# First unit of a seven-product feed-forward: weight sums split between GpSimd and VectorE, and the sixth product's left side built with one operation per token pair

## The chip, the cores and the metric

The kernel runs on one core of a Trainium2 chip, in one launch. The time is the device time of one execution in microseconds (us); the kernel before takes 2167.95 us, the median of three runs (2166.27 to 2169.98). Engines are named as in the profile: PE is TensorE (PEld its weight loads), DVE is VectorE, ACT is ScalarE, POOL is GpSimd, SP is SyncE, which issues most of the transfers.

## The reference, cut to what matters

Two layers of a decoder trunk on 512 tokens of width 1024, all float32:

```python
for l in range(DEPTH):                                   # DEPTH = 2
    x = x + 0.5 * swiglu_ffn(rmsnorm(x, ffn1_norm[l]), ffn1_w_gate[l], ffn1_w_up[l], ffn1_w_down[l])
    z = rmsnorm(x, mix_norm[l]) @ w_in[l]                # -> S5, pooling and conv groups -> y
    x = x + y @ w_out[l]
    x = x + cross_attention(rmsnorm(x, xattn_norm[l]), rmsnorm(mem, mem_norm[l]), wq, wk, wv, wo)
    x = x + 0.5 * swiglu_ffn(rmsnorm(x, ffn2_norm[l]), ffn2_w_gate[l], ffn2_w_up[l], ffn2_w_down[l])
return rmsnorm(x, final_norm)

def rmsnorm(x, g):
    return x * rsqrt(mean(x * x, axis=-1) + EPS) * g
def swiglu_ffn(h, w_gate, w_up, w_down):                 # 1024 -> 2816 -> 1024
    return (silu(h @ w_gate) * (h @ w_up)) @ w_down
```

The change concerns three of the four feed-forward blocks: `ffn2` of both layers and `ffn1` of the second. The first block of the program is built in another way and is not touched.

## The kernel before

Every float32 matrix product is done as three products of rounded parts: an operand is split into a high part (ScalarE copies it to `F32R`) and a rest (VectorE subtracts), and `mm3` (L300 to L302) adds high x high, rest x high and high x rest. So each weight tile costs one ScalarE and one VectorE operation before TensorE can use it (`split2`, L441 and L443 for a whole 128x1024 tile, L451 and L452 for a 128x512 one).

`ffn7` computes gate and up together with seven products of half-sized blocks in place of eight (a Strassen form). It goes over six *units* of up to 512 hidden columns. In a unit the weights stand in four quarters `raw[kh, z]`: `kh` is the half of the 1024 input channels, `z` is 0 for gate and 1 for up; each quarter is two tiles of 128x1024 (`quarter`, L655, two transfers of 512 KB). The products need sums of quarters: `t1` = (0,0) + (0,1) in four 128x512 operations (`mix1`, L472), then in place (0,1) += (1,1) and (0,0) += (0,1) (`mix2`) and (1,0) += (0,0) (`mix3`), two 128x1024 operations each (L476). The activations stand as four blocks, token half by channel half, A11, A12 (token tiles 0 and 1) and A21, A22 (tiles 2 and 3), with S1 = A22 - A21 and combinations of these. Seven steps run in the order 1, 2, 5, 6, 3, 7, 4 (the number is `i` in `un.product`); products 1 and 2 need only A11 and A12, product 5 needs S1 and `t1`, product 6 the sum in (0,0). `split2` for a step is issued two steps ahead.

The start of such a stage lies inside the end of the one before. For each token tile `nxt.half(t, h)` is called behind the residual add: ScalarE squares and sums (L188), VectorE adds (L190), GpSimd takes the power -0.5 (L191), VectorE multiplies twice (L228, half a row each), and for tiles 2 and 3 subtracts for S1 (L233). `give` then transposes a block on TensorE (L249), copies the high part on ScalarE (L251) and forms the rest on VectorE (L252). `combine(i)` builds the left sides of products 6, 3, 7 and 4, once per pair of token tiles (L240, L241, L243). `join` (L508) adds two products.

In the first unit of a stage (`u == 0`) the sums run on GpSimd (`self.eng`): `mix1` two steps early, `mix2` and `mix3` behind the last power of the norm, which `tc.issue_after(norm.pow)` demands. In the later units all sums run on VectorE. The order of instructions in each engine's queue is set by the Tile framework's scheduler from the order of the code and its own estimate of times; each engine runs its queue in order. The quarters of the first unit are loaded by `PairNorm.take`, which is called before the tail of the preceding stage.

## Time and profile before

| | us |
|---|---|
| median of three runs | 2167.95 |
| the profiled execution | 2170.75 |
| its span | 2168.9 |
| TensorE busy in the span | 2074.1 (96%) |
| VectorE busy | 1574.8 (73%) |
| ScalarE busy | 916.0 (42%) |
| GpSimd busy | 387.5 (18%) |
| mean granted clock of TensorE | 0.978 |

The profile is one execution, with every instruction's start and duration. Starts are counted from the start of the span; 1.85 us of the execution lie outside it. The granted clock is 1.00 at 2.4 GHz and 0.50 at 1.2 GHz. Durations of instructions that follow each other closely overlap by some hundredths of a microsecond. The three starts of seven-product stages lie in the span at about 705 to 770 us (behind the first attention), 1085 to 1135 (behind a feed-forward) and 1765 to 1830 (behind the second attention).

### The profile page before, as it was taken

What the parts mean: (1) busy time and instruction counts of PE and PEld (TensorE: products, weight loads), DVE (VectorE), ACT (ScalarE), POOL (GpSimd) and SP (SyncE); (2) the same over time, 40 slices, a digit from 0 to 9 for tenths busy, and PEclk for the clock granted to TensorE, in tenths of its full rate; (3) what the DMA queues carried; (4) which work ended last, traced back from release to release, by engine and by line L of the source; (5) the groups of instructions that cost most, each with busy time, mean ns of one, the idle gap of its engine ahead of it and who ended that gap; (6) DMA issues with size and microseconds to landing.
All of it is one profiled execution on the core that took longest, in us unless ns stands there. A gap on an engine that the chain in (4) does not pass through costs nothing.

```text
span 2168.9 us, 27451 instructions
## 1 busy us (share of the span) xinstructions
PE 2074.1 (96%) x10180; PEld 1737.9 (80%) x10180; DVE 1574.8 (73%) x2562; ACT 916.0 (42%) x1528; POOL 387.5 (18%) x361
## 2 busy tenths in 40 slices
...
GB/s 169 98 103 93 111 164 175 69 146 114 141 68 98 58 88 115 109 117 78 136 20 145 88 79 107 78 233 88 126 127 99 69 126 75 101 112 84 78 63 91
DMA packets 226749, 229.91 MB, mean 106 GB/s; under 512 B 38478, under 2 KB 152888, under 8 KB 226616
## 3 DMA queue, kind: packets, MB, share of 16 engines
...
HBM read 213.77 MB, written 12.58 MB: 104 GB/s over the span
## 4 chain that ended last, share of the span: by engine, by line
PE 79%; DVE 14%; ACT 2%; DMA 2%; issue 2%; SPq 0%; POOL 0%; DVEq 0%; POOLq 0%; ACTq 0%
PE pxffn L301 5%; PE pxffn L302 5%; PE pxffn L300 5%; PE pddffn L301 5%; PE pddffn L302 5%; PE pddffn L300 5%; DVE cacc L1052 3%; PE pzffn L300 3%; PE pzffn L301 3%; PE pzffn L302 3%; PE pgffn L301 2%; PE pgffn L300 2%; PE pgffn L302 2%; PE puffn L302 2%; PE puffn L300 2%
## 5 line engine op out<-in xcount | busy, mean ns | idle before, releaser
L301 PE MATMUL pddffn<-wl_dffn,hhffn 128*128 128x512 f32 x480 | 188.9, 394 | 0.0
L302 PE MATMUL pddffn<-wh_dffn,hlffn 128*128 128x512 f32 x480 | 188.2, 392 | 0.0
L300 PE MATMUL pddffn<-wh_dffn,hhffn 128*128 128x512 f32 x480 | 185.8, 391 | 0.0
L1052 DVE SCALAR_TENSOR_TENSOR cacc<-ch,convw,cacc 128x510 f32<-128x510 f32 (+28 forms) x174 | 127.9, 735 | 5.7 <-ACT cacc L1050 2.0
L367 DVE SCALAR_TENSOR_TENSOR x<-pddffn,x 128x512 f32<-128x512 f32 x120 | 82.5, 687 | 66.6 <-PE pddffn L302 66.6
L472 POOL TENSOR_TENSOR wt_ffn<-wr_first_ffn,wr_first_ffn 128x512 f32<-128x512 f32 x12 | 17.3, 1473 | 495.4 <-DMA wr_first_ffn<-in_ffn_w_up_dram 308.8
L301 PEld LDWEIGHTS pddffn<-wl_dffn,hhffn 128*128 128x128 f32 x480 | 90.2, 188 | 18.3
L302 PEld LDWEIGHTS pddffn<-wh_dffn,hlffn 128*128 128x128 f32 x480 | 90.2, 188 | 17.9
L300 PEld LDWEIGHTS pddffn<-wh_dffn,hhffn 128*128 128x128 f32 x480 | 89.8, 188 | 18.4
L476 DVE TENSOR_TENSOR wr_ffn<-wr_ffn,wr_ffn 128x1024 f32<-128x1024 f32 (+1 forms) x90 | 98.5, 1112 | 0.1
L293 POOL TENSOR_TENSOR wl_pl<-wr_pl,wh_pl 128x1024 fp32r<-128x1024 f32 x4 | 9.5, 2397 | 478.4 <-ACT wh_pl L291 478.4
L529 ACT ACTIVATE hhffn<-htffn 128x512 fp32r<-128x512 f32 x60 | 35.6, 594 | 80.8 <-PE htffn L523 80.6
L452 DVE TENSOR_TENSOR wl_dffn<-wr_dffn,wh_dffn 128x512 fp32r<-128x512 f32 x60 | 42.1, 705 | 36.8 <-PE pxffn L301 13.7
L300 PE MATMUL pgffn<-xh_ffn,wh_gffn 128*128 128x512 f32 x168 | 66.2, 394 | 0.0
L301 PE MATMUL pgffn<-xl_ffn,wh_gffn 128*128 128x512 f32 x168 | 66.0, 393 | 0.0
L302 PE MATMUL pgffn<-xh_ffn,wl_gffn 128*128 128x512 f32 x168 | 65.9, 393 | 0.0
L302 PE MATMUL puffn<-xh_ffn,wl_uffn 128*128 128x512 f32 x168 | 65.8, 392 | 0.0
L300 PE MATMUL puffn<-xh_ffn,wh_uffn 128*128 128x512 f32 x168 | 65.8, 392 | 0.0
L301 PE MATMUL puffn<-xl_ffn,wh_uffn 128*128 128x512 f32 x168 | 65.8, 392 | 0.0
L191 POOL TENSOR_TENSOR ss_final<-ss_final,nhalf 128x1 f32<-128x1 f32 x4 | 2.2, 548 | 345.1 <-DVE ss_final L190 345.1
L293 POOL TENSOR_TENSOR wl_v<-wr_v,wh_v 128x1024 fp32r<-128x1024 f32 x22 | 53.4, 2436 | 36.4 <-ACT wh_v L291 27.7
L300 PE MATMUL pdffn<-wh_dffn,h_ffffn 128*128 128x512 f32 x144 | 57.0, 396 | 1.5 <-DVE sffn L387 1.5
...
## 6 DMA issues: line engine op xcount, KB each, us to landing
...
```

Source lines behind the costliest of these rows:

```text
L191: self.pow = G.tensor_tensor(out=ss[:, 3:4], in0=ss[:, 2:3], in1=nhalf[:, 0:1], op=ALU.pow).ins
L293: (eng or V).tensor_tensor(out=lo, in0=raw, in1=h.bitcast(F32), op=SUB)
L300: T.matmul(ps, lhsT=wh, rhs=ah, start=first, stop=False, skip_group_check=skip)
L301: T.matmul(ps, lhsT=wh, rhs=al, start=False, stop=False, skip_group_check=skip)
L302: T.matmul(ps, lhsT=wl, rhs=ah, start=False, stop=last, skip_group_check=skip)
L367: V.scalar_tensor_tensor(out=x_, in0=ps, scalar=scale, in1=x_, op0=MUL, op1=ADD)
L452: V.tensor_tensor(out=lo, in0=r, in1=h.bitcast(F32), op=SUB)
L472: self.eng.tensor_tensor(out=t1[k], in0=a[k // 2][:, k % 2, :], in1=b[k // 2][:, k % 2, :], op=ADD)
L476: self.eng.tensor_tensor(out=a, in0=b, in1=a, op=ADD)
L529: A.activation(out=h, in_=pt, func=AF.Copy)
L1052: V.scalar_tensor_tensor(out=acc[:, d:], in0=h[:, 0:S - d], scalar=cw[:, TAPS - 1 - d:TAPS - d], in1=acc[:, d:], op0=MUL, op1=ADD)
```

## The change

For the first unit of a stage `take` now issues `t1` and the first in-place sum, (0,1) += (1,1), on GpSimd, at once behind the loads and so ahead of the stage's powers; (0,0) += (0,1) and (1,0) += (0,0) go to VectorE, at steps 1 and 2. The rule that sums stand behind the last power is gone. `combine(6)` now makes one operation per token pair, in place over S1, where it made two, one of them over A11; A21 = A11 - A21 is formed in `combine(7)`, and `combine(3)` reads the new tile. The later units are as before, with `self.eng` replaced by VectorE.

```diff
@@ -188,7 +188,7 @@
             A.activation(out=sq, in_=xt[t][:, dsl(h)], func=AF.Square, scale=D ** -0.5, accum_out=ss[:, h:h + 1])
             if h == 1:
                 V.tensor_scalar(out=ss[:, 2:3], in0=ss[:, 0:1], scalar1=ss[:, 1:2], scalar2=EPS, op0=ADD, op1=ADD)
-                self.pow = G.tensor_tensor(out=ss[:, 3:4], in0=ss[:, 2:3], in1=nhalf[:, 0:1], op=ALU.pow).ins
+                G.tensor_tensor(out=ss[:, 3:4], in0=ss[:, 2:3], in1=nhalf[:, 0:1], op=ALU.pow)
                 for i in range(2):
                     self.emit(t, i, ss[:, 3:4])
 
@@ -215,6 +215,12 @@
         def take(self):
             for kh, z in ((0, 0), (1, 0), (0, 1), (1, 1)):
                 self.raw[kh, z] = quarter(self.w[z], kh, z, 0, 4 * P, f"first_{self.name}")
+            a, b, d = self.raw[0, 0], self.raw[0, 1], self.raw[1, 1]
+            t1 = self.raw["t1"] = [vt(f"wt_first_{self.name}{k}") for k in range(HK)]
+            for k in range(HK):
+                G.tensor_tensor(out=t1[k], in0=a[k // 2][:, k % 2, :], in1=b[k // 2][:, k % 2, :], op=ADD)
+            for s in range(2):
+                G.tensor_tensor(out=b[s], in0=d[s], in1=b[s], op=ADD)
             self.xg = {}
             for i, z in ((1, "h"), (2, "l"), (5, "h"), (6, "l")):
                 t2 = xgp.tile([P, 2, HK, HS], F32R, tag=f"x{z}", name=f"xc_{self.name}{i}")
@@ -237,11 +243,12 @@
             for tp in range(2):
                 a11, a12, a21, a22, s1 = (self.xn[z] for z in ((tp, 0), (tp, 1), (tp + 2, 0), (tp + 2, 1), (tp + 2, 2)))
                 if i == 6:
+                    V.scalar_tensor_tensor(out=s1, in0=s1, scalar=-1.0, in1=a11, op0=MUL, op1=SUB)
+                elif i == 3:
+                    V.scalar_tensor_tensor(out=a12, in0=a12, scalar=-1.0, in1=s1, op0=MUL, op1=SUB)
+                elif i == 7:
                     V.tensor_tensor(out=a21, in0=a11, in1=a21, op=SUB)
-                    V.scalar_tensor_tensor(out=a11, in0=s1, scalar=-1.0, in1=a11, op0=MUL, op1=SUB)
-                elif i == 3:
-                    V.scalar_tensor_tensor(out=a12, in0=a12, scalar=-1.0, in1=a11, op0=MUL, op1=SUB)
-                self.give(tp, i, {6: a11, 3: a12, 7: a21, 4: a22}[i])
+                self.give(tp, i, {6: s1, 3: a12, 7: a21, 4: a22}[i])
 
         def give(self, tp, i, src):
             ps = ax(f"xp_{self.name}{tp}{i}", (P, HK, P))
@@ -460,7 +467,6 @@
                 self.W = self.nf * P
                 self.nm = f"{which}{l}_{u}"
                 self.raw, self.ps, self.e, self.ht = {}, {}, {}, {}
-                self.eng = V if u else G
 
             def load(self, kh, z):
                 self.raw[kh, z] = quarter((wg, wu)[z], kh, z, self.f0 * P, self.W, self.nm)
@@ -469,11 +475,11 @@
                 a, b = self.raw[0, 0], self.raw[0, 1]
                 t1 = self.raw["t1"] = [vt(f"wt_{self.nm}{k}", (P, self.W)) for k in range(HK)]
                 for k in range(HK):
-                    self.eng.tensor_tensor(out=t1[k], in0=a[k // 2][:, k % 2, :], in1=b[k // 2][:, k % 2, :], op=ADD)
+                    V.tensor_tensor(out=t1[k], in0=a[k // 2][:, k % 2, :], in1=b[k // 2][:, k % 2, :], op=ADD)
 
             def sum_(self, to, other):
                 for a, b in zip(self.raw[to], self.raw[other]):
-                    self.eng.tensor_tensor(out=a, in0=b, in1=a, op=ADD)
+                    V.tensor_tensor(out=a, in0=b, in1=a, op=ADD)
 
             def mix2(self):
                 self.sum_((0, 1), (1, 1))
@@ -570,17 +576,12 @@
             if u == 0:
                 for j, i in enumerate((6, 3, 7, 4)):
                     when(j + 1, lambda i=i: norm.combine(i))
-            lead = 2 if u == 0 else 0
-            when(-lead, un.mix1)
             if u == 0:
-                def behind(f):
-                    with tc.issue_after(norm.pow):
-                        f()
-                when(1 - lead, lambda: behind(us[0].mix2))
-                when(2 - lead, lambda: behind(us[0].mix3))
+                when(1, lambda: us[0].sum_((0, 0), (0, 1)))
             else:
+                when(0, un.mix1)
                 when(1, un.mix2)
-                when(2, un.mix3)
+            when(2, un.mix3)
             final = u + 1 == len(us)
             if u > 0:
                 us[u - 1].down(0)
```

Lines of the changed kernel below L221 are 6 or 7 higher than those of the kernel before: L228 becomes L234, L233 L239, L252 L259, L365 L372, L443 L450, L452 L459, L476 L482, L508 L514. L240 and L241 become L250 and L246, L243 becomes L248, and L472 becomes L221 in the first unit. In the names, `xn` are normalised half rows, `xs` is S1, `xc` are transposed parts, `wr_first_ffn` are the first unit's quarters (6337 and 6339 the two tiles of (0,0), 6341 and 6343 of (1,0), 6345 and 6347 of (0,1), 6349 and 6351 of (1,1)), `wt` is `t1` and `wl` the rest of a split weight; `x_101` to `x_104` are the token tiles, `pwo_tc` a result of the attention's output projection for token tile t and column half c.

GpSimd at the first start, the kernel before:

```order
L472 TENSOR_TENSOR wt_ffn_02_6568<-wr_first_ffn_6339,wr_first_ffn_6347 128x512
L472 TENSOR_TENSOR wt_ffn_03_6569<-wr_first_ffn_6339,wr_first_ffn_6347 128x512
L191 TENSOR_TENSOR ss_ffn_6370<-ss_ffn_6370,nhalf 128x1
L191 TENSOR_TENSOR ss_ffn_6409<-ss_ffn_6409,nhalf 128x1
L191 TENSOR_TENSOR ss_ffn_6467<-ss_ffn_6467,nhalf 128x1
L191 TENSOR_TENSOR ss_ffn_6520<-ss_ffn_6520,nhalf 128x1
L476 TENSOR_TENSOR wr_first_ffn_6345<-wr_first_ffn_6349,wr_first_ffn_6345 128x1024
L476 TENSOR_TENSOR wr_first_ffn_6347<-wr_first_ffn_6351,wr_first_ffn_6347 128x1024
L476 TENSOR_TENSOR wr_first_ffn_6337<-wr_first_ffn_6345,wr_first_ffn_6337 128x1024
L476 TENSOR_TENSOR wr_first_ffn_6339<-wr_first_ffn_6347,wr_first_ffn_6339 128x1024
L476 TENSOR_TENSOR wr_first_ffn_6341<-wr_first_ffn_6337,wr_first_ffn_6341 128x1024
L476 TENSOR_TENSOR wr_first_ffn_6343<-wr_first_ffn_6339,wr_first_ffn_6343 128x1024
```

and now:

```order
L221 TENSOR_TENSOR wt_first_ffn_6355<-wr_first_ffn_6339,wr_first_ffn_6347 128x512
L221 TENSOR_TENSOR wt_first_ffn_6356<-wr_first_ffn_6339,wr_first_ffn_6347 128x512
L223 TENSOR_TENSOR wr_first_ffn_6345<-wr_first_ffn_6349,wr_first_ffn_6345 128x1024
L223 TENSOR_TENSOR wr_first_ffn_6347<-wr_first_ffn_6351,wr_first_ffn_6347 128x1024
L191 TENSOR_TENSOR ss_ffn_6380<-ss_ffn_6380,nhalf 128x1
L191 TENSOR_TENSOR ss_ffn_6419<-ss_ffn_6419,nhalf 128x1
L191 TENSOR_TENSOR ss_ffn_6477<-ss_ffn_6477,nhalf 128x1
L191 TENSOR_TENSOR ss_ffn_6530<-ss_ffn_6530,nhalf 128x1
L221 TENSOR_TENSOR wt_first_ffn_9532<-wr_first_ffn_9516,wr_first_ffn_9524 128x512
L221 TENSOR_TENSOR wt_first_ffn_9533<-wr_first_ffn_9516,wr_first_ffn_9524 128x512
```

The six sums behind the four powers are gone; two of them stand ahead of the powers.

VectorE at the first start, around the first token tile's normalising operations, the kernel before:

```order
L365 TENSOR_TENSOR x_101<-pwo_01_6296,x_101 128x512
L365 TENSOR_TENSOR x_102<-pwo_10_6145,x_102 128x512
L190 TENSOR_SCALAR ss_ffn_6370<-ss_ffn_6370 128x1
L228 SCALAR_TENSOR_TENSOR xn_ffn_6384<-x_101,ss_ffn_6370,gb_ffn_6333 128x512
L228 SCALAR_TENSOR_TENSOR xn_ffn_6393<-x_101,ss_ffn_6370,gb_ffn_6334 128x512
L365 TENSOR_TENSOR x_102<-pwo_11_6412,x_102 128x512
L365 TENSOR_TENSOR x_103<-pwo_20_6146,x_103 128x512
L190 TENSOR_SCALAR ss_ffn_6409<-ss_ffn_6409 128x1
```

and now:

```order
L372 TENSOR_TENSOR x_101<-pwo_01_6296,x_101 128x512
L372 TENSOR_TENSOR x_102<-pwo_10_6145,x_102 128x512
L190 TENSOR_SCALAR ss_ffn_6380<-ss_ffn_6380 128x1
L482 TENSOR_TENSOR wr_first_ffn_6339<-wr_first_ffn_6347,wr_first_ffn_6339 128x1024
L372 TENSOR_TENSOR x_102<-pwo_11_6422,x_102 128x512
L234 SCALAR_TENSOR_TENSOR xn_ffn_6394<-x_101,ss_ffn_6380,gb_ffn_6333 128x512
L234 SCALAR_TENSOR_TENSOR xn_ffn_6403<-x_101,ss_ffn_6380,gb_ffn_6334 128x512
L372 TENSOR_TENSOR x_103<-pwo_20_6146,x_103 128x512
L190 TENSOR_SCALAR ss_ffn_6419<-ss_ffn_6419 128x1
```

The sum into tile 6339 stands ahead of the second half of `x_102` and of the first tile's normalising operations.

VectorE at the first start, from the last token tile's normalising operations on, the kernel before:

```order
L243 SCALAR_TENSOR_TENSOR xn_ffn_6393<-xn_ffn_6393,xn_ffn_6384 128x512
L228 SCALAR_TENSOR_TENSOR xn_ffn_6553<-x_104,ss_ffn_6520,gb_ffn_6333 128x512
L228 SCALAR_TENSOR_TENSOR xn_ffn_6555<-x_104,ss_ffn_6520,gb_ffn_6334 128x512
L252 TENSOR_TENSOR xc_ffn_6355<-xp_ffn_6506,xc_ffn_6355 128x4x128
L233 TENSOR_TENSOR xs_ffn_6557<-xn_ffn_6555,xn_ffn_6553 128x512
L240 TENSOR_TENSOR xn_ffn_6553<-xn_ffn_6442,xn_ffn_6553 128x512
L241 SCALAR_TENSOR_TENSOR xn_ffn_6442<-xs_ffn_6557,xn_ffn_6442 128x512
L243 SCALAR_TENSOR_TENSOR xn_ffn_6451<-xn_ffn_6451,xn_ffn_6442 128x512
L508 TENSOR_TENSOR u1ffn_00_6646<-pyffn_00_6680,u1ffn_00_6646 128x512
L508 TENSOR_TENSOR u1ffn_01_6648<-pyffn_01_6681,u1ffn_01_6648 128x512
L252 TENSOR_TENSOR xc_ffn_6355<-xp_ffn_6559,xc_ffn_6355 128x4x128
L452 TENSOR_TENSOR wl_ffn_0p_6605<-wt_ffn_00_6566,wh_ffn_0p_6604 128x512
```

and now:

```order
L190 TENSOR_SCALAR ss_ffn_6530<-ss_ffn_6530 128x1
L246 SCALAR_TENSOR_TENSOR xs_ffn_6514<-xs_ffn_6514,xn_ffn_6394 128x512
L234 SCALAR_TENSOR_TENSOR xn_ffn_6563<-x_104,ss_ffn_6530,gb_ffn_6333 128x512
L234 SCALAR_TENSOR_TENSOR xn_ffn_6565<-x_104,ss_ffn_6530,gb_ffn_6334 128x512
L259 TENSOR_TENSOR xc_ffn_6365<-xp_ffn_6516,xc_ffn_6365 128x4x128
L248 SCALAR_TENSOR_TENSOR xn_ffn_6403<-xn_ffn_6403,xs_ffn_6514 128x512
L239 TENSOR_TENSOR xs_ffn_6567<-xn_ffn_6565,xn_ffn_6563 128x512
L514 TENSOR_TENSOR u1ffn_00_6642<-pyffn_00_6676,u1ffn_00_6642 128x512
L250 TENSOR_TENSOR xn_ffn_6563<-xn_ffn_6452,xn_ffn_6563 128x512
L514 TENSOR_TENSOR u1ffn_01_6644<-pyffn_01_6677,u1ffn_01_6644 128x512
L246 SCALAR_TENSOR_TENSOR xs_ffn_6567<-xs_ffn_6567,xn_ffn_6452 128x512
L259 TENSOR_TENSOR xc_ffn_6365<-xp_ffn_6569,xc_ffn_6365 128x4x128
```

The operation that writes S1's tile (`xs_ffn_6514`, then `xs_ffn_6567`) has taken the place of the one that wrote A11's, and the first of the two stands ahead of the last tile's normalising operations; A21 is formed ahead of it (L250) and A12 behind it (L248).

## Rows read from the trace of the kernel before

**Rows 1.** The page, section 1: busy us, share of the span, instructions.

```profile
PE 2074.1 (96%) x10180; PEld 1737.9 (80%) x10180; DVE 1574.8 (73%) x2562; ACT 916.0 (42%) x1528; POOL 387.5 (18%) x361
```

**Rows 2.** Busy time by stretch: us, PE, PEld, DVE, ACT, POOL, PEclk, DMA, GB/s.

```profile
745.00:770.00 25.00, 13.62 (x58) 10.31 (x57) 24.46 (x24) 10.00 (x17) 12.99 (x5) 0.73 0.03 4
1110.00:1135.00 25.00, 16.34 (x58) 11.76 (x57) 24.73 (x25) 9.27 (x17) 12.84 (x5) 0.73 0.00 0
1804.00:1829.00 25.00, 13.62 (x53) 10.27 (x52) 23.90 (x22) 8.89 (x16) 13.23 (x5) 0.73 0.02 3
```

**Rows 3.** Timeline of VectorE, first start: start, us, engine, line, operation, [idle before].

```profile
733.84 1.41 DVE L228 SCALAR_TENSOR_TENSOR xn_ffn<-x,ss_ffn,gb_ffn 128x512 f32<-128x512 f32 x2
...
737.50 1.22 DVE L443 TENSOR_TENSOR wl_ffn_0p<-wr_first_ffn,wh_ffn_0p 128x1024 fp32r<-128x1024 f32 x1
...
741.81 5.67 DVE L228 SCALAR_TENSOR_TENSOR xn_ffn<-x,ss_ffn,gb_ffn 128x512 f32<-128x512 f32 x2 [0.44 <-POOL ss_ffn L191]
747.41 0.68 DVE L252 TENSOR_TENSOR xc_ffn<-xp_ffn,xc_ffn 128x512 fp32r<-128x512 f32 x1
748.01 2.26 DVE L233 TENSOR_TENSOR xs_ffn<-xn_ffn,xn_ffn 128x512 f32<-128x512 f32 x1
...
753.06 2.73 DVE L241 SCALAR_TENSOR_TENSOR xn_ffn<-xs_ffn,xn_ffn 128x512 f32<-128x512 f32 x1
```

**Rows 4.** GpSimd: L476's durations (ns, min/median/max), and its timeline at the first start.

```profile
L476 POOL TENSOR_TENSOR wr_first_ffn<-wr_first_ffn,wr_first_ffn x18: 2392/2812/2850, 741.7 to 1814.4; 128x1024 f32<-128x1024 f32 x18
...
709.54 5.95 POOL L472 TENSOR_TENSOR wt_ffn<-wr_first_ffn,wr_first_ffn 128x512 f32<-128x512 f32 x4 [93.44 <-DVE l_o L309]
718.25 0.55 POOL L191 TENSOR_TENSOR ss_ffn<-ss_ffn,nhalf 128x1 f32<-128x1 f32 x1 [2.76 <-DVE ss_ffn L190]
...
740.91 0.86 POOL L191 TENSOR_TENSOR ss_ffn<-ss_ffn,nhalf 128x1 f32<-128x1 f32 x1 [7.26 <-DVE ss_ffn L190]
741.75 16.24 POOL L476 TENSOR_TENSOR wr_first_ffn<-wr_first_ffn,wr_first_ffn 128x1024 f32<-128x1024 f32 x6
```

**Rows 5.** Timeline of TensorE at the three starts: around products 1, 2 and 6.

```profile
737.01 0.61 PE L300 MATMUL pxffn<-wh_ffn_0p,xc_ffn 128*128 128x512 f32 x2
...
748.16 0.39 PE L302 MATMUL pyffn<-wh_ffn_0p,xc_ffn 128*128 128x512 f32 x1
...
763.32 1.22 PE L301 MATMUL pxffn<-wl_ffn_0p,xc_ffn 128*128 128x512 f32 x2 [0.34 <-DVE wl_ffn_0p L443]
...
1115.72 0.50 PE L302 MATMUL pyffn<-wh_ffn_0p,xc_ffn 128*128 128x512 f32 x1 [2.43 <-DVE xc_ffn L252]
...
1129.98 1.22 PE L301 MATMUL pxffn<-wl_ffn_0p,xc_ffn 128*128 128x512 f32 x2 [0.94 <-DVE wl_ffn_0p L443]
...
1807.39 0.39 PE L302 MATMUL pyffn<-wh_ffn_0p,xc_ffn 128*128 128x512 f32 x1
...
1822.57 1.22 PE L301 MATMUL pxffn<-wl_ffn_0p,xc_ffn 128*128 128x512 f32 x2 [0.34 <-DVE wl_ffn_0p L443]
```

**Rows 6.** Instructions by line and shape: VectorE's own sums in later units.

```profile
L476 DVE TENSOR_TENSOR wr_ffn<-wr_ffn,wr_ffn 128x1024 f32<-128x1024 f32 x72 | 86.7, 1218 | 0.0
```

**Rows 7.** Busy time by stretch, columns as in the second group.

```profile
715.00:720.00 5.00, 5.00 (x23) 4.14 (x23) 3.36 (x6) 2.17 (x6) 1.04 (x2) 1.00 0.00 0
1078.00:1079.00 1.00, 1.00 (x7) 0.87 (x6) 1.00 (x3) 1.00 (x3) 0.00 (x0) 1.00 0.95 369
1085.00:1095.00 10.00, 10.00 (x48) 8.20 (x46) 3.83 (x7) 0.38 (x1) 0.00 (x0) 1.00 0.12 43
```

**Rows 8.** Waits of VectorE in 715 to 765: us, times, longest.

```profile
DVE x L365 <- PE pwo L302: 9.1, 7, 3.2
```

**Rows 9.** Single microseconds, columns as in the second group (PEclk third from the end).

```profile
765.00:766.00 1.00, 1.00 (x4) 0.86 (x3) 1.00 (x3) 0.56 (x2) 0.00 (x0) 0.52 0.00 0
1134.00:1135.00 1.00, 1.00 (x7) 0.96 (x6) 0.73 (x2) 0.07 (x1) 0.00 (x0) 0.70 0.00 0
1827.00:1828.00 1.00, 1.00 (x6) 0.91 (x6) 0.32 (x1) 0.34 (x1) 0.00 (x0) 0.75 0.00 0
```

## The prediction

> **What bounds the kernel now.** The page first: TensorE is busy 96% of the span [rows 1], so time can come only from places where it waits or runs at its lower clock. The change touches three, the starts of the seven-product stages near 745, 1110 and 1804 us. The table by stretches is read next: in 25 us at each start TensorE is busy 13.62, 16.34 and 13.62 us at a mean granted clock of 0.73, while VectorE is busy 24.46, 24.73 and 23.90 [rows 2]. VectorE is the engine to follow there.
>
> Its timeline says why it is full. At the first start the two normalising operations of one token tile (L228) take 1.41 us together at 733.84 and 5.67 us at 741.81; behind them L233, L240, L241 and L243 on 128x512 take 2.26 to 2.73 us each, two of them shown [rows 3]. In the same stretch L252, which reads PSUM and one SBUF tile, takes 0.68 [rows 3]. GpSimd runs its six 128x1024 sums in these 16.24 us from 741.75, right behind the last tile's power at 740.91 [rows 4]. A slow operation takes about as long as a GpSimd sum (2812 ns median, 2392 the shortest [rows 4]). I read this as the two engines taking turns when both read two SBUF operands. The Trainium skill, "SBUF — State Buffer", section "Who interferes with whom", says the same: such a VectorE instruction contends with a GpSimd instruction that reads SBUF, and whichever issues later waits for all of the other. The rows agree, L252 included.
>
> Then TensorE's timeline: products 1 and 2 end at 748.4, and product 6 runs without waits only from 763.32, after a split (L443) [rows 5]. At the third start the same two points are 1807.6 and 1822.57. At the second, product 2 itself meets a wait of 2.43 us, and product 6 runs from 1129.98 [rows 5].
>
> **The change part by part.**
>
> *Sums leave the place behind the last power.* Six operations per start go from there. GpSimd keeps the four for t1 and two for the (0,1) sum, all ahead of the stage's powers; four 128x1024 sums go to VectorE, 1218 ns each by its own rows [rows 6], in a row of others 1.14, since successive operations overlap by 0.08 (747.41 to 748.01 is 0.60 for one of 0.68 [rows 3]): 4.6 us per start.
>
> *GpSimd's queue.* At the first start t1 runs 709.54 to 715.5 [rows 4]; two sums of 2.39 to 2.81 end at 720.3 to 721.1, and the first power, due at 718.25 [rows 4], stands behind them, 2 to 3 us late. All traffic has ended by 715 [rows 7], so the weights are there. On VectorE the first sum (the second pair of fences of the change) waits for GpSimd's second sum, and behind it stand a residual add, itself waiting for TensorE, and the two L228 of the first tile: they end near 724.8, some 4.6 us later than now. TensorE has the output projection until 737.0 [rows 5], and its new order takes that tile's transposes near 729, behind two thirds of it. Price 0 while that cover is there; without it 4.6 us. The second start has its last weight at 1079 (369 GB/s in 1078 to 1079 [rows 7]); GpSimd is then done by 1082, and it has nothing to do in 1085 to 1095 [rows 7]: price 0. At the third the first start's figures return.
>
> *Four sums in VectorE's queue.* Between 715 and 765 VectorE waits 9.1 us for the projection's results [rows 8], and in 1085 to 1095 it is busy 3.83 of 10 us [rows 7]; so about half of the 4.6 us falls into waiting. From 733 on the queue is full, and there two sums (2.3 us) stand where L241 and L243 stood (1.2 us less). Adding the queue up from the first start's rows (0.60 per 128x512 operation, 1.14 per 128x1024), I get the last tile's power at 743.0 instead of 740.91.
>
> *The sixth product.* Six operations per start as before; one per pair moves to the seventh. The new form writes over S1, so L246 (lines from here to the sum are the changed kernel's, L228 apart) must wait until TensorE has transposed S1, a wait that the old form had not. At the first start L246 of the first pair stands ahead of the last tile's L228 in VectorE's queue; those transposes come behind twelve matmuls of product 2, near 744.0, so L228 starts near 744.8 instead of 743.9: 0.9 us for the whole queue behind it. The second pair's L246 waits for transposes that stand behind product 2.
>
> *The sum.* TensorE executes the same instructions up to the end of product 2, and waits for nothing there at the first and third start, so that end stays at 748.4 and 1807.6. What remains behind it is VectorE's queue, eight operations of the changed order: L514, L246, L259, L459, L248, two L459, then the 128x1024 split for product 6. That is 7 x 0.60 + 1.14 = 5.3 us, 0.2 for the first hand-over, and the queue reaches that point 0.7 us late at the first start and 0.5 at the third. TensorE's gap of 763.3 - 748.4 = 14.9 us becomes 6.2 and 6.0: 8.7 and 8.9 saved. At the second start the wait inside product 2 goes too; by the same adding up product 2 ends near 1116, 5.3 us of queue follow, and product 6 runs from 1121.3: 8.7 saved. Together 26.3.
>
> *The clock.* At the first start it is back from 0.50 (1.2 GHz) to 1.00 at 766.0 (mean 0.52 in that microsecond), at the second at 1134.6 (0.70), at the third at 1827.5 (0.75) [rows 9]; product 6 thus runs 2.7, 4.6 and 4.9 us at half speed, and half of that is lost: 6.1 us. In the new gap of 6 us TensorE still does 1.4 us of transposes; the rows of before show it falling in gaps of 15 us, and say nothing of one of 6. So the return lies between 0 and 6.1; I take half, 3.0.
>
> Sum: 26.3 + 3.0 = 29.3 us. The profiled execution took 2170.75 (span 2168.9), 2.8 above the median; that gives 2141.4 for such an execution, and 2167.95 - 29.3 = 2138.7, rounded 2139, for the median.
>
> **A rule against it.** At the second start GpSimd's second sum (1079 to 1082) meets VectorE's splits and its own first sum, all with two SBUF operands. By rows 3 that costs VectorE up to two waits of 2.1 us (2.73 instead of 0.60), and VectorE has 6.2 us free in 1085 to 1095, so my sum has 0. The Trainium skill's "SBUF — State Buffer" ("Who interferes with whom") makes the later one wait for all of the other; with that cover gone the sum would be 29.3 - 4.2 = 25.1.
>
> **The rivals.**
> 1. *VectorE becomes the bound.* The sums and L246's wait bring the last tile's norm later than I added up. If the queue reaches the point behind product 2 some 5 us late instead of 0.7, each start saves 4.5 and the clock falls as before: 13.5, 2154. For it: VectorE's 24 of 25 us [rows 2]. Against: 9.1 us of waiting just ahead [rows 8].
> 2. *The clock stays up.* All 6.1 come back, 26.3 + 6.1 = 32.4: 2135.6.
> 3. *Slower: the powers stand behind a weight.* The sum that now precedes all four powers needs the last quarter of the up weights. Up to a landing near 721 at the first start the projection covers it; beyond, every microsecond goes into the norm, and at 730 the 8.7 are used up; a landing at 735 would cost 5 at each start: 2183. Rows 7 speak against it: traffic ends by 715 and 1079, and the order of SyncE's queue does not change.
> 4. *Nothing moves.* The slow operations had another cause than GpSimd and come again: 2168. Against it: L228 at 1.41 and 5.67 us within 8 us of each other, and L252 untouched [rows 3].
>
> **How the numbers follow.** Forecast 0.66 (own range 2135 to 2145: the clock's two ends, and 2 us per start for the queue), rival 1 0.13, rival 2 0.14, rival 3 0.03, rival 4 0.04. The range holds the forecast and rival 2, some 4 us more below, and reaches half way into rival 1: 2131 to 2150. A measurement of this kernel tells about 0.2% (4.3 us) from no change. Faster by more: the forecast, rivals 1 and 2, 0.93; within: rival 4, 0.04; slower: 0.03.
>
> **What would show it.** Right: no VectorE operation on 128x512 over 1.4 us between the last power and product 6 at any start; L228 of the last tile 1.4 us for both; GpSimd empty behind the fourth power; a gap near 6 us between product 2 and product 6, and product 2 as far behind the projection's end as now. L246's wait shows as idle time of VectorE that ends with TensorE's transposes. Wrong: a wait of VectorE for GpSimd's sum over 4 us; TensorE waiting inside products 1 and 2; a gap of 10 us or more; or the gain given back within the unit, with TensorE waiting for splits in products 5 to 4.

## The result: 1.1% faster, with the turns behind the last power gone and the clock not back

The changed kernel takes 2144.2 us (median of 4 runs, 2143.4 to 2146.8) where the kernel before took 2167.1 on the same chip (4 runs); the ratio is 0.9888, 95% interval 0.9876 to 0.9900. That is 22.9 us by the medians; the two profiled executions differ by 24.2 us (span 2144.7, and 2168.9 before). The forecast was 29.3 us.

The page first, section 1, against [rows 1]: TensorE's busy time is what it was, VectorE has 18.6 us less with 12 instructions more, GpSimd 30 us less.

```profile
PE 2073.3 (97%) x10180; PEld 1736.2 (81%) x10180; DVE 1556.2 (73%) x2574; ACT 915.5 (43%) x1528; POOL 357.4 (17%) x349
```

The table by stretches answers to [rows 2]; the second and third stretch are taken 7 and 15 us earlier, since the stages come earlier. In 25 us TensorE is now busy some 22 us instead of 13.6 to 16.3, and GpSimd half a microsecond or less instead of 13.

```profile
745.00:770.00 25.00, 22.18 (x93) 17.09 (x91) 19.32 (x30) 14.63 (x24) 0.51 (x1) 0.86 0.23 74
1103.00:1128.00 25.00, 22.38 (x95) 17.45 (x94) 18.62 (x29) 13.62 (x22) 0.00 (x0) 0.86 0.21 66
1789.00:1814.00 25.00, 21.67 (x98) 16.93 (x98) 21.24 (x31) 15.91 (x27) 0.31 (x1) 0.93 0.28 94
```

VectorE's timeline at the first start, against [rows 3]. L234 is the normalising operation (L228 before), L246, L248 and L250 form the operands, L514 adds a product's result, L459 and L450 split weights.

```profile
745.57 0.69 DVE L246 SCALAR_TENSOR_TENSOR xs_ffn<-xs_ffn,xn_ffn 128x512 f32<-128x512 f32 x1 [0.69 <-PE xp_ffn L256]
746.18 1.41 DVE L234 SCALAR_TENSOR_TENSOR xn_ffn<-x,ss_ffn,gb_ffn 128x512 f32<-128x512 f32 x2
...
750.50 0.69 DVE L514 TENSOR_TENSOR u1ffn<-pyffn,u1ffn 128x512 f32<-128x512 f32 x1
751.10 0.69 DVE L246 SCALAR_TENSOR_TENSOR xs_ffn<-xs_ffn,xn_ffn 128x512 f32<-128x512 f32 x1
751.70 0.69 DVE L259 TENSOR_TENSOR xc_ffn<-xp_ffn,xc_ffn 128x512 fp32r<-128x512 f32 x1
752.30 0.69 DVE L459 TENSOR_TENSOR wl_ffn_0p<-wt_first_ffn,wh_ffn_0p 128x512 fp32r<-128x512 f32 x1
752.90 0.69 DVE L248 SCALAR_TENSOR_TENSOR xn_ffn<-xn_ffn,xs_ffn 128x512 f32<-128x512 f32 x1
753.50 1.29 DVE L459 TENSOR_TENSOR wl_ffn_0p<-wt_first_ffn,wh_ffn_0p 128x512 fp32r<-128x512 f32 x2
754.71 1.23 DVE L450 TENSOR_TENSOR wl_ffn_0p<-wr_first_ffn,wh_ffn_0p 128x1024 fp32r<-128x1024 f32 x1
```

The last tile's normalising pair takes 1.41 us instead of 5.67, every 128x512 operation here 0.69. The turns are gone from this place only: ahead of the powers, beside t1 and the two sums, single splits of VectorE still take 1.77 us (at 712.37) and 2.58 (at 1067.38). The last seven rows are the eight operations that the prediction counted behind product 2, in its order: 750.50 to 755.94, 5.4 us.

GpSimd at the first start, against [rows 4]: t1, the two sums, and the first and last of the four powers. Behind the last power there is nothing.

```profile
709.35 5.94 POOL L221 TENSOR_TENSOR wt_first_ffn<-wr_first_ffn,wr_first_ffn 128x512 f32<-128x512 f32 x4 [91.79 <-DMA wr_first_ffn<-in_ffn_w_up_dram]
715.25 4.76 POOL L223 TENSOR_TENSOR wr_first_ffn<-wr_first_ffn,wr_first_ffn 128x1024 f32<-128x1024 f32 x2
719.97 0.55 POOL L191 TENSOR_TENSOR ss_ffn<-ss_ffn,nhalf 128x1 f32<-128x1 f32 x1
...
744.96 0.55 POOL L191 TENSOR_TENSOR ss_ffn<-ss_ffn,nhalf 128x1 f32<-128x1 f32 x1 [8.06 <-DVE ss_ffn L190]
```

TensorE around product 2's last matmul and product 6's first unbroken matmuls, against [rows 5], first, second and third start:

```profile
749.73 0.39 PE L309 MATMUL pyffn<-wh_ffn_0p,xc_ffn 128*128 128x512 f32 x1
749.96 1.03 PE L256 MATMUL xp_ffn<-ident,xs_ffn 128*128 128x128 f32 x8
...
754.23 0.80 PE L307 MATMUL pxffn<-wh_ffn_0p,xc_ffn 128*128 128x512 f32 x1 [1.06 <-ACT xc_ffn L258]
...
755.99 1.22 PE L308 MATMUL pxffn<-wl_ffn_0p,xc_ffn 128*128 128x512 f32 x2
...
1114.60 1.22 PE L308 MATMUL pxffn<-wl_ffn_0p,xc_ffn 128*128 128x512 f32 x2
...
1794.06 0.39 PE L309 MATMUL pyffn<-wh_ffn_0p,xc_ffn 128*128 128x512 f32 x1
...
1800.16 1.10 PE L308 MATMUL pxffn<-wl_ffn_0p,xc_ffn 128*128 128x512 f32 x2
```

The gap, from product 2's end to product 6's first matmul with the rest of the weights (L308, L301 before), is 6.0 us at the first start (749.96 to 755.99), 5.5 at the second (1109.1 to 1114.60) and 5.9 at the third (1794.29 to 1800.16); it was 14.9, 8.8 and 15.0. In it the clock still falls. The granted clock (third number from the end) of stretches that lie in the gap's end and product 6:

```profile
754.00:761.00 7.00, 6.56 (x18) 4.70 (x19) 6.74 (x11) 4.37 (x9) 0.00 (x0) 0.52 0.00 0
1113.00:1119.00 6.00, 5.74 (x15) 3.83 (x16) 6.00 (x10) 3.89 (x8) 0.00 (x0) 0.50 0.00 0
1799.00:1802.00 3.00, 2.66 (x9) 1.94 (x9) 3.00 (x5) 3.00 (x7) 0.00 (x0) 0.50 0.00 0
```

### The profile page after: what moved, and what is told of

Same layout as the page of the kernel before. It is cut to its first block, busy times and chain, and to the rows that moved or that the text cites. A ratio compares the mean times of both kernels' runs of the same rounds, so it can differ in the third digit from the quotient of the medians.

```text
span 2144.7 us, 27458 instructions
## 1 busy us (share of the span) xinstructions
PE 2073.3 (97%) x10180; PEld 1736.2 (81%) x10180; DVE 1556.2 (73%) x2574; ACT 915.5 (43%) x1528; POOL 357.4 (17%) x349
## 4 chain that ended last, share of the span: by engine, by line
PE 80%; DVE 10%; ACT 3%; DMA 2%; issue 2%; POOL 1%; SPq 1%; DVEq 0%; POOLq 0%; ACTq 0%
PE pxffn L308 6%; PE pxffn L309 6%; PE pxffn L307 6%; PE pddffn L308 5%; PE pddffn L309 5%; PE pddffn L307 5%; DVE cacc L1053 3%; PE pzffn L307 3%; PE pzffn L308 3%; PE pzffn L309 3%; PE pdffn L307 2%; PE pdffn L309 2%; PE pdffn L308 1%; PE qps L308 1%; PE qps L309 1%
## 5 line engine op out<-in xcount | busy, mean ns | idle before, releaser
L308 PE MATMUL pddffn<-wl_dffn,hhffn 128*128 128x512 f32 x480 | 189.0, 394 | 0.0
L308 PEld LDWEIGHTS pddffn<-wl_dffn,hhffn 128*128 128x128 f32 x480 | 90.2, 188 | 18.3
L221 POOL TENSOR_TENSOR wt_first_ffn<-wr_first_ffn,wr_first_ffn 128x512 f32<-128x512 f32 x12 | 17.3, 1475 | 499.6 <-DMA wr_first_ffn<-in_ffn_w_up_dram 406.6
L482 DVE TENSOR_TENSOR wr_ffn<-wr_ffn,wr_ffn 128x1024 f32<-128x1024 f32 (+1 forms) x90 | 98.8, 1115 | 0.1
L459 DVE TENSOR_TENSOR wl_dffn<-wr_dffn,wh_dffn 128x512 fp32r<-128x512 f32 x60 | 42.1, 706 | 37.6 <-PE pxffn L308 16.7
L308 PE MATMUL pgffn<-xl_ffn,wh_gffn 128*128 128x512 f32 x168 | 66.0, 393 | 0.0
L308 PE MATMUL puffn<-xl_ffn,wh_uffn 128*128 128x512 f32 x168 | 65.8, 392 | 0.0
```

Source lines behind the costliest of these rows:

```text
L221: G.tensor_tensor(out=t1[k], in0=a[k // 2][:, k % 2, :], in1=b[k // 2][:, k % 2, :], op=ADD)
L308: T.matmul(ps, lhsT=wh, rhs=al, start=False, stop=False, skip_group_check=skip)
L459: V.tensor_tensor(out=lo, in0=r, in1=h.bitcast(F32), op=SUB)
L482: V.tensor_tensor(out=a, in0=b, in1=a, op=ADD)
```

## The experiments

All kernels together, for orientation. "At the starts" is what TensorE gains against the kernel before in the stretch around each start, from the two profiled executions compared matmul by matmul (fillings left out; the stretches are 712 to 844, 1100 to 1150 and 1775 to 1850 us of the kernel before); "half" is how many us around the three starts TensorE was granted 1.2 GHz, together. The ratio is that of the runs without profile to those of the kernel before on the same chip.

| kernel | median us | ratio, 95% interval | at the starts, us | sum | half |
|---|---|---|---|---|---|
| before | 2167 to 2170 | 1 | 0 | 0 | 41 |
| changed | 2144.2 | 0.9888 (0.9876 to 0.9900) | 7.5, 8.4, 11.0 | 26.9 | 17 |
| changed, once more | 2143.8 | 0.9879 (0.9861 to 0.9898) | 8.3, 9.1, 11.0 | 28.4 | 10 |
| only the sums moved | 2142.9 | 0.9879 (0.9863 to 0.9896) | 9.2, 8.9, 9.0 | 27.1 | 17 |
| only the sixth product | 2170.7 | 1.0010 (0.9999 to 1.0021) | -1.5, -0.6, -0.9 | -3.0 | 48 |
| ten additions put back | 2159.7 | 0.9959 (0.9947 to 0.9971) | 1.9, 5.0, 4.8 | 11.7 | 34 |
| 24 fills instead | 2143.2 | 0.9881 (0.9863 to 0.9899) | 8.3, 9.1, 11.0 | 28.4 | 10 |
| 14 operations, one operand | 2150.1 | 0.9911 (0.9890 to 0.9931) | 4.6, 8.0, 7.2 | 19.8 | 27 |
| no sums on VectorE | 2140.1 | 0.9878 (0.9865 to 0.9892) | 8.5, 11.6, 9.5 | 29.6 | 7 |
| all six sums on VectorE | 2140.0 | 0.9871 (0.9858 to 0.9885) | 9.2, 9.9, 10.1 | 29.2 | 10 |
| gap filled | 2133.5 | 0.9850 (0.9835 to 0.9865) | 10.2, 11.7, 11.4 | 33.3 | 0 |
| product 6 first | 2132.3 | 0.9839 (0.9826 to 0.9853) | 9.2, 9.3, 11.1 | 29.6 | 14 |
| both | 2128.6 | 0.9820 (0.9798 to 0.9843) | 10.7, 11.6, 11.7 | 34.0 | 0 |
| both, six sums on VectorE | 2133.2 | 0.9827 (0.9808 to 0.9847) | 10.9, 11.6, 11.7 | 34.2 | 0 |

### Which half of the change pays

Only the sums moved: the changed kernel with the old sixth product.

```diff
 if i == 6:
-    V.scalar_tensor_tensor(out=s1, in0=s1, scalar=-1.0, in1=a11, op0=MUL, op1=SUB)
+    V.tensor_tensor(out=a21, in0=a11, in1=a21, op=SUB)
+    V.scalar_tensor_tensor(out=a11, in0=s1, scalar=-1.0, in1=a11, op0=MUL, op1=SUB)
 ...
```

The part that is cut takes the branches for products 3 and 7 and the operand of `give` back to the old form too.

> The changed kernel with the sixth product's operands formed as before (three operations per token pair again, product 6 written over the first tile's half, nothing waits for the transposes of S1); only the sums stay moved. Taking turns (the theory): the whole gain comes from the sums that left GpSimd behind the last power, so the time is that of the changed kernel, 2144 us, within 3 us either way, and no VectorE operation on 128x512 takes over 1.4 us at the three starts; VectorE's 0.69 us wait for TensorE's transposes ahead of the last tile's normalising pair is gone, which is worth at most 0.7 us per start. Rival (the one operation that moved from the sixth to the seventh product carries a good part of the gain, since it leaves the queue behind product 2): the gap between products 2 and 6 is some 1.2 us longer at each start and the time 2148 us or more.

Only the sixth product: the kernel before with these lines taken the other way.

> The kernel before with nothing changed but the sixth product's form. Taking turns: GpSimd's six sums still run behind the last power beside VectorE's queue, so 128x512 operations with two SBUF operands still take 2.2 to 2.8 us and the gap stays near 12 to 15 us; 2160 to 2168 us. Rival (the shorter queue ahead of product 6 is what pays): the gap falls under 10 us and the time to 2155 us or less.

The sums alone bring the whole gain (0.9879, the changed kernel 0.9888 and 0.9879), the sixth product alone none (1.0010; its 2170.7 us lie above my 2160 to 2168, and its gaps of 15.4, 9.0 and 15.4 us are no shorter than those before). In the second kernel the turns are all there; its VectorE timeline at the first start:

```profile
739.24 5.68 DVE L228 SCALAR_TENSOR_TENSOR xn_ffn<-x,ss_ffn,gb_ffn 128x512 f32<-128x512 f32 x2 [0.73 <-POOL ss_ffn L191]
```

The two other theories, that the shorter queue pays or that the moved operation carries a part, fall: with the old form the gaps are 5.9, 4.7 and 5.8 us, not 1.2 longer. The small advantage that I gave the old form for having no wait on the transposes cannot be told in the time.

### Is it the turns, and whose operands make them

The changed kernel gets work that nobody needs, behind the last tile's power; `sq` is a dead 128x512 tile. On VectorE, TensorE and ScalarE the order stays as in the changed kernel.

```diff
-G.tensor_tensor(out=ss[:, 3:4], in0=ss[:, 2:3], in1=nhalf[:, 0:1], op=ALU.pow)
+pw = G.tensor_tensor(out=ss[:, 3:4], in0=ss[:, 2:3], in1=nhalf[:, 0:1], op=ALU.pow).ins
+if t == NT - 1 and isinstance(self, PairNorm):
+    with tc.issue_after(pw):
+        for _ in range(10):
+            G.tensor_tensor(out=sq, in0=sq, in1=sq, op=ADD)
```

> The changed kernel plus work that nobody needs: behind the last tile's power GpSimd adds a dead 128x512 tile to itself ten times (about 1.45 us each), so GpSimd is busy for some 15 us with two SBUF operands at the place where the six sums stood; no other engine's order changes and nothing waits for these additions. Taking turns: VectorE's 128x512 operations with two SBUF operands there take over 1.4 us again (at least twice the 0.69 of the changed kernel), those that read PSUM keep 0.69, the gap grows from 6 to 11 us or more at each start, and the time goes back by at least 15 of the 23 us: 2159 to 2172 us. Rival (what paid was that the weight sums come earlier, or that VectorE's queue is ordered otherwise): nothing waits for the additions, so 2144 us within 3.

The second kernel has `for _ in range(24): G.memset(sq, 0.0)` there.

> As the kernel with ten additions put back, but instead GpSimd fills the dead 128x512 tile with zeros 24 times: it is busy at the same place for a similar time (I do not know the time of one fill; 0.4 to 0.8 us by the nearest sizes), yet reads no SBUF operand. If the turns are taken between operations that read SBUF: VectorE's operations stay at 0.69 us and the time at 2144 us within 3. Rival (any GpSimd instruction beside VectorE slows it): 128x512 operations over 1.4 us and over 2155 us.

The third has `for _ in range(14): G.tensor_scalar(out=sq, in0=sq, scalar1=0.0, scalar2=None, op0=ADD)`.

> As the kernel with ten additions put back, but GpSimd's 14 operations on the dead 128x512 tile have one SBUF operand (tile plus a constant). If it takes a GpSimd operation with two SBUF operands to hold VectorE up: VectorE stays at 0.69 us per 128x512 and the time is 2144 us within 3, as it was with 24 fills that read nothing. If one operand is enough: 128x512 operations of 0.9 to 1.5 us, as beside the ten additions, and 2155 to 2165 us.

First start, the ten additions together and then two of them singly between VectorE's operations (L238, L243, L252 and L263 are here what L234, L239, L248 and L259 are in the changed kernel):

```profile
743.65 14.06 POOL L195 TENSOR_TENSOR sq_ffn<-sq_ffn 128x512 f32<-128x512 f32 x10
...
747.66 1.37 POOL L195 TENSOR_TENSOR sq_ffn<-sq_ffn 128x512 f32<-128x512 f32 x1
748.06 0.68 DVE L263 TENSOR_TENSOR xc_ffn<-xp_ffn,xc_ffn 128x512 fp32r<-128x512 f32 x1
748.66 0.92 DVE L252 SCALAR_TENSOR_TENSOR xn_ffn<-xn_ffn,xs_ffn 128x512 f32<-128x512 f32 x1
749.11 1.37 POOL L195 TENSOR_TENSOR sq_ffn<-sq_ffn 128x512 f32<-128x512 f32 x1
749.51 1.52 DVE L243 TENSOR_TENSOR xs_ffn<-xn_ffn,xn_ffn 128x512 f32<-128x512 f32 x1
```

24 fills:

```profile
744.85 13.93 POOL L195 MEMSET sq_ffn<- 128x512 f32 x24
...
745.58 1.41 DVE L238 SCALAR_TENSOR_TENSOR xn_ffn<-x,ss_ffn,gb_ffn 128x512 f32<-128x512 f32 x2
```

14 operations with one operand:

```profile
745.66 22.45 POOL L195 TENSOR_SCALAR sq_ffn<-sq_ffn 128x512 f32<-128x512 f32 x14
...
746.74 1.75 DVE L238 SCALAR_TENSOR_TENSOR xn_ffn<-x,ss_ffn,gb_ffn 128x512 f32<-128x512 f32 x2
```

Nothing waits for the additions, and yet they take back 16.5 us of the time (2143.2 with the fills, 2159.7 with the additions, on the same chip) and 15 to 17 of the 27 to 28 us at the starts. The gap grows to 11.9, 9.4 and 11.4 us; at the second start that is less than the 11 that I had put on it. The fills keep GpSimd busy as long (13.9 and 14.1 us) at no price that the time shows. So it is neither the order of VectorE's queue nor a busy GpSimd, but GpSimd's reading beside VectorE's operations that read two SBUF operands; L263, which reads PSUM, keeps 0.68 throughout.

My number for the additions was too simple: I wrote that such operations would take at least twice 0.69, and many take 0.92. The rows say why. L252, begun at 748.66, ends at 749.58, 0.55 us after the addition that was running when it began (747.66 to 749.03). L243, begun at 749.51, ends at 751.03, again 0.55 us after its addition (749.11 to 750.48). The same 0.55 stands behind all ten such operations of this start, and behind the 18 that met a sum at the three starts of the kernel before. So VectorE waits until the addition is over: L243 for nearly all of one, L252 for the end of one, because L263 came between. GpSimd waits too: the first addition, with nothing to wait for, takes 1.04 us, the nine others 1.37. Beside sums of 2.4 to 2.8 us VectorE's operations took 2.2 to 2.9, beside the additions 0.92 to 1.53.

With one operand the price is smaller still (0.68 to 1.10, gaps of 8.5, 6.4 and 8.0 us, 2150.1 us), between the two answers that I had laid out. There the operations that wait end some 0.33 us before GpSimd's instruction does, so they did not wait for all of it.

The Trainium skill, "SBUF — State Buffer", section "Who interferes with whom", says that such a VectorE operation contends with a GpSimd instruction that reads SBUF and not with one that only writes it. The three kernels agree with that. It also calls the shared ports an exclusive lock, by which the later one waits for all of the other. With two operands on GpSimd the rows agree with this too (the 0.55 us above); with one operand they don't (the 0.33 us).

### Do VectorE's own sums cost anything

Left out: the changed kernel's four sums on VectorE.

```diff
 if u == 0:
-    when(1, lambda: us[0].sum_((0, 0), (0, 1)))
+    pass
 ...
-when(2, un.mix3)
+if u:
+    when(2, un.mix3)
```

> The changed kernel without VectorE's four sums of the first unit (left out: the sums that products 6 and 4 of that unit need, so these two products use other weights; everything else stands). The prediction had half of the four sums' 4.6 us fall into VectorE's waiting and the two that stand after 733 in the full queue, 2.3 us per start. By that the last tile's power comes up to 2.3 us earlier and the gap between products 2 and 6 shrinks by 1 to 2.3 us at the first and third start: 2137 to 2142 us where the changed kernel has 2144. Rival (the sums are hidden, because product 2 and the queue behind it set the gap, eight operations that no sum precedes): 2144 us within 2.

All six on VectorE: the kernel before with `V` for `self.eng` in `sum_`; GpSimd keeps t1.

> The kernel before with one change: the first unit's six sums on VectorE instead of GpSimd (GpSimd keeps t1, as before; the sixth product's form is the old one). They are no longer tied to the last power, and four of the six stand ahead of it in VectorE's queue. Taking turns: no 128x512 operation of VectorE over 1.4 us behind the power; VectorE carries 6 x 1.14 = 6.8 us instead of 4.6 in the changed kernel, of which up to 2.3 more may stand in the full queue: 2144 to 2151 us. Rival (VectorE is the bound, so that six sums in its queue cost what the turns had cost): 2160 us or more.

Without the sums GpSimd's last power comes at 741.81 instead of 744.96, but that moves the gap little. VectorE then waits for product 2, and what follows is the same queue:

```profile
748.90 1.44 DVE L514 TENSOR_TENSOR u1ffn<-pyffn,u1ffn 128x512 f32<-128x512 f32 x2 [1.64 <-PE pyffn L309]
...
753.86 1.22 DVE L450 TENSOR_TENSOR wl_ffn_0p<-wr_first_ffn,wh_ffn_0p 128x1024 fp32r<-128x1024 f32 x1
```

The transposes behind product 2 begin at 749.38 and product 6 runs from 755.14, 5.8 us against 6.0; at the third start it is 6.1 against 5.9. The ratio, 0.9878, is that of the changed kernel (0.9888 and 0.9879). The median of 2140.1 us lies in my first range, but it comes from a chip on which the changed kernel would take 2141 to 2143 by its ratios. So the rival holds at these two starts: the sums are hidden. At the second start the gap does shrink, from 5.5 to 4.3 us, and there the clock does not fall. The kernel with six sums on VectorE says it from the other side; 6.8 us of them per start cost nothing (0.9871, under the 2144 to 2151 that I had expected). All six of them, and not four, begin ahead of the last power there, at 716 to 741 us. GpSimd was not needed for the two sums that it keeps.

### The clock, and what else sets the gap

Filled gap: dead transposes behind those of product 6's operand.

```diff
-    T.transpose(ps[:, k, :], src[:, k * P:(k + 1) * P], ident)
+    mv = T.transpose(ps[:, k, :], src[:, k * P:(k + 1) * P], ident)
+if i == 6:
+    if tp == 0:
+        self.fill = cx(f"fill_{self.name}", (P, HK, P))
+    with tc.issue_after(mv.ins):
+        for k in range((12, 8)[tp]):
+            T.transpose(self.fill[:, k % HK, :], ident, ident)
```

> The changed kernel with work for TensorE that nobody needs: behind the first pair's transposes of product 6's operand 12 transposes of the identity into a free PSUM tile, behind the second pair's 8 more (0.13 us each, 1.6 and 1.0 us), in the gap in which TensorE waits for VectorE and ScalarE. In the changed kernel product 6 runs 5.0, 4.6 and 2 us at 1.2 GHz at the three starts, which costs half of that, 5.8 us together. If the fall of the clock follows from the idle gap: it stays at 1.00 through product 6, the three starts lose at most 0.5 us each to the filling, and the time is 2139 to 2142 us. Rival (the clock falls all the same, or the filling delays product 6 by as much as it returns): 2143 to 2146 us.

Its clock at the first start, in the gap and in product 6, and one stretch at each of the others:

```profile
749.00:753.00 4.00, 3.75 (x33) 3.31 (x31) 4.00 (x7) 3.46 (x6) 0.00 (x0) 1.00 0.01 2
753.00:758.00 5.00, 4.07 (x19) 2.83 (x20) 5.00 (x9) 4.51 (x10) 0.00 (x0) 1.00 0.00 0
...
1110.00:1115.00 5.00, 4.66 (x23) 3.51 (x24) 5.00 (x9) 4.07 (x8) 0.00 (x0) 1.00 0.00 0
...
1785.00:1790.00 5.00, 4.06 (x20) 2.66 (x19) 5.00 (x9) 4.53 (x9) 0.00 (x0) 1.00 0.00 0
```

It stays at 2.4 GHz at all three, and the starts gain 5 to 6.4 us over the two profiles of the changed kernel, about the 5.8 that I had put on it. Beside the kernel before on the same chip the time fell by 6 to 8 us more than the changed kernel's (0.9850 against 0.9888 and 0.9879), where I had expected 2 to 5. So the starts are most of it, and each interval is about 3 us wide to either side. The profiled executions differ by 13 us; the 7 to 8 us beyond the starts lie in stages that the filling does not touch, where this execution had fewer stretches at 1.2 GHz. Whether the filling has a part in that I cannot say.

Product 6 first: the two lines change places for the first unit. The sum that product 6 needs comes one step earlier, and `combine` of products 3, 7 and 4 one step later.

```diff
-un.product("z", 5, True, False, "t1", un.keep("z", "u5"))
+five = lambda: un.product("z", 5, True, False, "t1", un.keep("z", "u5"))
+if u:
+    five()
 un.product("x", 6, False, False, (0, 0), un.keep("x", "u2"))
+if u == 0:
+    five()
 ...
-    for j, i in enumerate((6, 3, 7, 4)):
+    for j, i in zip((0, 2, 3, 4), (6, 3, 7, 4)):
 ...
-    when(1, lambda: us[0].sum_((0, 0), (0, 1)))
+    when(0, lambda: us[0].sum_((0, 0), (0, 1)))
```

> The changed kernel with product 6 of the first unit ahead of product 5 in the program, so that VectorE and ScalarE split product 6's weights ahead of product 5's three splits, which stand in the gap now although TensorE runs product 6 first. If VectorE's queue behind product 2 sets the gap, three operations of 0.60 us leave it: 1.2 to 1.8 us less at each start, the time 2138 to 2141 us. Rival (something else ends the gap, the transposes of product 6's operand and ScalarE's part of the split, or product 5 now waits for what product 6 had waited for): 2143 to 2147 us.

Faster by more than expected (0.9839), but hardly by the mechanism that I gave. VectorE's split L450 now comes 2.9 us behind product 2 instead of 4.8, and product 6's first matmul with its result (L308) 4.6 us instead of 6.0, within the 1.2 to 1.8 that I had counted. Yet product 6 begins as late as it did, and meets another wait:

```profile
751.01 1.21 DVE L450 TENSOR_TENSOR wl_ffn_0p<-wr_first_ffn,wh_ffn_0p 128x1024 fp32r<-128x1024 f32 x1
```

```profile
748.07 1.03 PE L256 MATMUL xp_ffn<-ident,xs_ffn 128*128 128x128 f32 x8
...
752.34 0.50 PE L307 MATMUL pxffn<-wh_ffn_0p,xc_ffn 128*128 128x512 f32 x1 [1.07 <-ACT xc_ffn L258]
752.67 0.40 PE L308 MATMUL pxffn<-wl_ffn_0p,xc_ffn 128*128 128x512 f32 x1
...
754.69 0.80 PE L309 MATMUL pxffn<-wh_ffn_0p,xc_ffn 128*128 128x512 f32 x1 [0.61 <-DVE xc_ffn L259]
```

From the eight transposes to product 6's first matmul it is 4.27 us, as in the changed kernel (749.96 to 754.23): the operand's own way, transposes, VectorE, ScalarE. And where the split no longer holds TensorE up, the rest of the operand does (L259), until 754.69. So the queue to the split was not the only way that ends so late. The stretches behind the first and third start gain up to 1 us each, where TensorE had waited 0.8 and 0.4 us for ScalarE's copy of product 5 (L509) and now does not. Starts and stretches together gain 31.1 us, against 26.9 and 28.4 in the two profiles of the changed kernel. That is some 3 to 4 of the 9 to 11 us (0.9839 against 0.9879 and 0.9888); the rest stays open, as for the filling.

Both edits together, and with all six sums on VectorE besides:

> Both edits that were faster than the changed kernel together: product 6 of the first unit ahead of product 5 in the program, and the 12 and 8 transposes of the identity for TensorE in the gap. The first alone took 2132.3 us, the second 2133.5. If they act on different things (the clock in the gap; the order of splits and products in the unit), the clock stays at 1.00 through product 6 at all three starts and the time is 2122 to 2129 us. Rival (they return the same microseconds, or what they returned was clock falls elsewhere that other executions do not repeat): 2130 to 2136 us.

> As the kernel with product 6 first and the filled gap, and GpSimd's two sums of the first unit on VectorE too (six there, GpSimd keeps t1). The kernel before with all six on VectorE took 2140.0 us, somewhat less than the changed kernel. If the two sums ahead of GpSimd's powers cost something (the first power came 1.7 us later), 2 to 4 us less than the kernel without this edit. If their delay is covered by the projection, as the prediction had it, and VectorE's two further sums fall into its waiting: the same within 2 us. Rival (VectorE's queue is what sets the last tile's norm): 2 to 7 us more.

With 2128.6 us (0.9820) the two together have the lowest time here, 15 us under the changed kernel on the same chip; the interval overlaps with that of product 6 first alone. The clock stays at 1.00 at all three starts, and at the starts the filling does nearly all (33.3 us without the other order, 34.0 with it). With the two sums on VectorE the median is 4.6 us higher, which is the rival's answer, but the ratios (0.9827 and 0.9820) and the starts (34.2 and 34.0) cannot be told apart, and the five executions without this edit lie between 2125 and 2138 us. So the time shows no cost of GpSimd's two sums ahead of its powers, as the prediction had it.

### The changed kernel once more

> The changed kernel itself, unaltered, on the same chip as the other kernels of this call, to compare them with it and to see which of its clock falls ahead of the starts (at 707 and 1751 us in its first profile) another execution repeats. 2142 to 2147 us. If the falls are chance, at least one of the two is absent in the new profile; if the change brings them, both are there.

In the changed kernel's first profile TensorE runs at 1.2 GHz near 707 and 1751, behind a wait of 2.13 us in the attention stage (it ends at 705.05 and 1749.42) that the kernel before has too, without a fall there. First profile, then the second one, where these waits end at 707.55 and 1748.87:

```profile
707.00:708.00 1.00, 1.00 (x4) 0.78 (x3) 0.53 (x1) 0.95 (x2) 0.00 (x0) 0.50 1.04 404
1751.00:1754.00 3.00, 3.00 (x9) 2.35 (x8) 1.89 (x3) 1.96 (x4) 0.30 (x1) 0.50 1.05 408
```

```profile
710.00:712.00 2.00, 2.00 (x11) 1.65 (x10) 1.93 (x4) 1.76 (x4) 0.15 (x1) 1.00 1.06 410
1751.00:1754.00 3.00, 3.00 (x9) 2.31 (x9) 2.16 (x4) 2.07 (x5) 0.91 (x1) 0.54 1.05 407
```

The first fall is gone, the second is there again. Both lie ahead of the first sum that the change touches (GpSimd's t1 begins at 709.35 and at 1753.70), and each costs an execution some 1.6 us. Of the ten profiles in which GpSimd has its two sums ahead of the powers two show the first fall and five the second; of the four others (before, only the sixth product, and the two with six sums on VectorE) none. The first is therefore not the change's alone, and for the second five of ten against none of four is too little to tell chance from cause. That stays open.

## Why the prediction was right, and what it mis-sized

**The mechanism and the queue: right.** GpSimd's sums and VectorE's operations take turns, the sums leave, the turns end. The prediction's three terms against the first profile, TensorE's lead at that place taken off (it came to the first start 1.6 us late, to the second 6.6 and to the third 13.3 us early):

- first start, forecast 8.7: product 6 from 763.32 to 755.99, 7.3 + 1.6 = 8.9;
- second, 8.7: 1129.98 to 1114.60, 15.4 - 6.6 = 8.8;
- third, 8.9: 1822.57 to 1800.16, 22.4 - 13.3 = 9.1.

That is 26.8 of 26.3 (at the third start the gap of 15.0 us would have given 9.0 in the forecast, not 8.9). The queue behind product 2 took 5.4 us of 5.3 and began 0.5 late instead of 0.7; the wait of L246 was 0.69 of 0.9; the last power came at 744.96, which is 743.4 with TensorE's 1.6 us taken off, of 743.0. Product 2's end moved only with TensorE's delay.

**The clock: mis-sized.** I had taken half of 6.1 us, 3.0, as coming back. From [rows 9] product 6 ran 2.7, 4.6 and 4.9 us at half speed, 12.2 together; now it is 5.1, 4.9 and 2.0, 12.0 (5.0, 4.6 and 2 in the expectation for the filled gap were read too short). Half of the difference, 0.1 us, came back. The gap is shorter, but the clock falls in it all the same, and since product 6 begins earlier, more of it lies in the slow stretch at the first start. In the second profile of the changed kernel product 6 runs 3.4, 3.4 and 2.0 us at half speed, 8.8, which returns 1.7. So the term varies with the execution, 0.1 and 1.7 in the two seen, and the 3.0 lies above both. Rival 2, the whole 6.1, takes an edit that fills the gap; with it the starts gave 33 us.

**What had no term.** The falls at 707 and 1751 took 1.6 and 1.7 us in the profiled execution. 26.8 + 0.1 - 3.3 = 23.6, of the measured 24.2. A forecast from one execution contains that execution's falls elsewhere, and they come and go.

**Costed at nothing, and rightly.** The first power came 1.7 us later (719.97), the first tile's L234 at 724.86 to 726.3, which is 724.7 with TensorE's delay taken off, of 724.8, and TensorE did not wait. VectorE waits 7.8 us for the projection between 715 and 765 where it waited 9.1 [rows 8]:

```profile
DVE x L372 <- PE pwo L309: 7.8, 5, 3.0
```

I had split the four sums into a half that falls into waiting and a half that stands in the full queue; the kernel without them shows that the second half delays the last tile's norm too, but that norm has slack before product 2's end.

**The rule against it** (second start) did meet VectorE, and here the price fell to GpSimd. The changed kernel, then the one with only the sums moved:

```profile
1074.80 5.63 POOL L223 TENSOR_TENSOR wr_first_ffn<-wr_first_ffn,wr_first_ffn 128x1024 f32<-128x1024 f32 x1 [5.39 <-DMA wr_first_ffn<-in_ffn_w_up_dram]
1075.76 1.22 DVE L450 TENSOR_TENSOR wl_ffn_0p<-wr_first_ffn,wh_ffn_0p 128x1024 fp32r<-128x1024 f32 x1
1080.46 1.23 DVE L482 TENSOR_TENSOR wr_first_ffn<-wr_first_ffn,wr_first_ffn 128x1024 f32<-128x1024 f32 x1 [1.36 <-POOL wr_first_ffn L223]
```

```profile
1073.17 3.41 DVE L449 TENSOR_TENSOR wl_ffn_0p<-wr_first_ffn,wh_ffn_0p 128x1024 fp32r<-128x1024 f32 x1
...
1078.44 0.50 PE L306 MATMUL pddffn<-wh_dffn,hhffn 128*128 128x512 f32 x1 [1.47 <-DVE x L373]
```

In the changed kernel the sum takes 5.63 us instead of 2.4, VectorE's split its usual 1.22; VectorE then waits 1.36 us for the sum, with 12 us until the next power. That was luck in part: in eight of the ten profiles that have the sum here GpSimd paid in this way, and in two VectorE did. With only the sums moved its split took 3.41 us, one wait of 2.2 such as the rule counts, and TensorE waited 1.47 us for a residual add behind it (ahead of the stretch that the table counts); without VectorE's own sums a 128x512 split took 2.87 and TensorE waited 0.33. So the 0 in the sum held for the changed kernel, but not for certain. The last weight landed at 1074.8, later against the stage than the forecast's 1079 (1072.4 with the 6.6 us taken off), and the cover held.

**The other rivals.** VectorE as the bound (rival 1) fell with the kernels that give it no sums and six sums: the time goes with neither. Slower (rival 3) did not come near: GpSimd ends its sums at 720 and 1080.4. That nothing moves (rival 4) fell with the additions put back.
